# Seven-product SwiGLU pairs on one Trainium2 core: the first weight sum in two buffers of its own, and the second sum placed behind a named VectorE instruction

## The chip, the cores and the metric

The kernel runs on one core of a Trainium2 chip. The metric is device time in microseconds (us), the median of the runs shown. TensorE (PE in the profile) does the matmuls; VectorE (DVE), ScalarE (ACT) and GpSimd (POOL) each take their instructions strictly in the order in which they were queued; SP and POOL issue the transfers used here.

## The reference

A trunk of two layers over 512 tokens of width 1024, all float32. Each layer is an attention or delta-rule mixer between two half-step SwiGLU blocks, each behind an RMS norm. The part that matters here is the SwiGLU:

```python
def swiglu(h, w_gate, w_up, w_down):
    return (jax.nn.silu(h @ w_gate) * (h @ w_up)) @ w_down

for layer in range(DEPTH):          # DEPTH = 2, D_MODEL = 1024, D_FF = 2816
    x = x + 0.5 * swiglu(rms_norm(x, ffn1_norm[layer]), ffn1_w_gate[layer], ffn1_w_up[layer], ffn1_w_down[layer])
    ...                             # mixer
    x = x + 0.5 * swiglu(rms_norm(x, ffn2_norm[layer]), ffn2_w_gate[layer], ffn2_w_up[layer], ffn2_w_down[layer])
```

## The kernel before

**Blocks and pairs.** Four SwiGLU blocks run (`ffn`). Each walks the 22 column blocks of the hidden width in pairs, by groups. In the first three SwiGLU blocks the groups hold 6, 8 and 8 column blocks: the first three pairs are computed plainly (`eight`), the other eight pairs, four in each of the two later groups, by `seven`. After each group comes a down projection (`add_out`). So there are 3 x 8 = 24 pairs made by `seven`, in six groups of four. The fourth SwiGLU block doesn't use `seven`.

**The seven products.** `seven` makes a 2x2 block product with seven multiplications (a Winograd form). The halves of the depth and of the two column blocks give weight quarters; sums of quarters are formed on the way: t1 and t3 by a plain load from SP followed by an accumulating load from POOL into the same tile, t2 = t1 + b22 and t4 = t2 + b21 on VectorE (L511 and L522). Every product first splits its weights into a high and a low part (ACT cast `wh` L225, DVE subtraction `wl` L226, three buffers each) and then runs 24 matmuls of 128x256 (L498). The order of the products on TensorE is: 0 into X (b11), 1 into Y (t2), 2 into Z (t1), 3 added to Y (t3), 4 added to X (b21), 5 added to Y (t4), 6 added to Z (b22). In the profile X is an `mm` tile, Y a `pa` tile, Z a `pb` tile; `sb` is b11, `sr` holds b21 and b22.

**Reads between the products.** Y and Z are read by VectorE between products that add to them: u2 = p1 + Y after product 1 (L514), u3 = p1 + Y after product 3 (L518), c22 = Z - u3 (L504, named `gr`). Product 5 may not start on Y before u3 has read it, product 6 not on Z before c22 has. "The fourth product" below is product 3.

**Buffers.** t1, t3, t2, t4 of every pair, and the down projection's panels too, take the next of three `raw` buffers in turn, so in the kernel before t1 of the next pair can be loaded only when the buffer of the present pair's t3 is free.

**Order.** The instructions of the next pair are mixed into those of the present one by a scheduler, which sets one fixed order for each engine and each queue; `issue_after(i)` makes what stands under it come behind instruction i in that order. The norm of each SwiGLU block needs a small power on POOL (`rt`, L159) before its row scale `rb` (L299) can be made.

Of the kernel before, what the change touches and what calls it, by code (L numbers as in the profile page):

```python
# [10 lines left out]
F32 = mybir.dt.float32  # L11
F32R = mybir.dt.float32r
AF = mybir.ActivationFunctionType
ALU = mybir.AluOpType

P = 128
# [84 lines left out]
class Trunk:  # L101
# [328 lines left out]
    def quarters(self, pool):  # L430

        nc = self.nc
        tags = [(self.xp, f"xn{p}{c}") for c in range(KC) for p in "hl"]
        tags += [(pool, f"sx{i}") for i in range(12)]
        norm = []
        for kh in range(2):
            t = pool.tile([P, 4 * T], F32, tag="sr", name="xr")
            for k in range(4):  # L440
                c = kh * 4 + k
                nc.vector.scalar_tensor_tensor(t[:, k * T:(k + 1) * T], self.x[c],
                                               self.gain[:, c:c + 1], self.rb, ALU.mult, ALU.mult)
            norm.append(t.rearrange("p (k t) -> p k t", k=4))
        self.left = [[[], []] for _ in range(7)]
        v2 = lambda t: t.rearrange("p (k t) -> p k t", k=2)
        for i in range(2):
            a = [[norm[kh][:, 2 * i:2 * i + 2, t * 256:(t + 1) * 256] for kh in range(2)]
                 for t in range(2)]
            s1, s2, s3, s4 = (v2(self.small(pool, t)) for t in ("gr", "sg", "ur", "hd"))  # L450
            tt = nc.vector.tensor_tensor
            tt(s1, a[1][0], a[1][1], op=ALU.subtract)
            tt(s2, s1, a[0][0], op=ALU.subtract)
            tt(s3, a[0][0], a[1][0], op=ALU.subtract)
            tt(s4, a[0][1], s2, op=ALU.add)
            for o, src in enumerate((a[0][0], s2, s1, s3, a[0][1], a[1][1], s4)):
                h, l = (v2(pl.tile([P, T], F32R, tag=tag, name=tag, bufs=1))
                        for pl, tag in (tags.pop(0), tags.pop(0)))
                self.split_to(h, l, src)
                self.left[o][0].append(h)  # L460
                self.left[o][1].append(l)

    def seven(self, pool, wg, wu, f):

        nc = self.nc
        x8 = lambda t: t.rearrange("p (x c) -> p x c", x=8)
        def load(eng, v, kh, lo, hi, **kw):
            for q, w in enumerate((wg, wu)):  # L470
                eng.dma_start(v[:, q * 4:q * 4 + 4], w[kh * 512:(kh + 1) * 512,  # L471
                                                       f * P + lo:f * P + hi]
                              .rearrange("(k p) c -> p k c", p=P), **kw)
        raw = lambda: x8(self.wp.tile([P, 1024], F32, tag="raw", name="raw", bufs=NRAW))
        add = dict(accum_op=ALU.add)
        b11 = x8(pool.tile([P, 1024], F32, tag="sb", name="sb"))
        load(nc.sync, b11, 0, 0, P)
        b2 = x8(pool.tile([P, 2048], F32, tag="sr", name="sr"))
        load(nc.sync, b2, 1, 0, 2 * P)
        t1, t3 = raw(), raw()  # L480
        load(nc.sync, t1, 0, 0, P)
        load(nc.gpsimd, t1, 0, P, 2 * P, **add)
        load(nc.sync, t3, 0, P, 2 * P)
        load(nc.gpsimd, t3, 1, P, 2 * P, **add)
        b21, b22 = b2[:, :, :P], b2[:, :, P:]
        X, Y, Z = self.mm_ps(), self.a_ps(), self.b_ps()

        def product(ps, o, right, start=False):
            h = x8(self.wp.tile([P, 1024], F32R, tag="wh", name="wh", bufs=NSPL))
            l = x8(self.wp.tile([P, 1024], F32R, tag="wl", name="wl", bufs=NSPL))  # L490
            self.split_to(h, l, right)
            ah, al = self.left[o]
            for q in range(2):
                out = ps[:, q * 256:(q + 1) * 256]
                for k in range(4):
                    a = [t[k // 2][:, k % 2] for t in (ah, al)]
                    for i, (wt, xt) in enumerate(((h, a[0]), (h, a[1]), (l, a[0]))):
                        nc.tensor.matmul(out, lhsT=wt[:, q * 4 + k], rhs=xt,  # L498
                                         start=start and q + k + i == 0,
                                         stop=q == 1 and k == 3 and i == 2, skip_group_check=True)  # L500

        def combine(tag, a, b, op):
            t = self.small(pool, tag)
            nc.vector.tensor_tensor(t, a, b, op=op)  # L504
            return t

        product(X, 0, b11, True)
        p1 = self.np_.tile([P, T], F32, tag="acc", name="p1", bufs=1)
        nc.scalar.copy(out=p1, in_=X)
        t2 = raw()  # L510
        nc.vector.tensor_tensor(t2, t1, b22, op=ALU.add)  # L511
        product(Y, 1, t2, True)
        u2 = self.np_.tile([P, T], F32, tag="sq", name="u2")
        nc.vector.tensor_tensor(u2, p1, Y, op=ALU.add)  # L514
        product(Z, 2, t1, True)
        product(Y, 3, t3)
        u3 = self.np_.tile([P, T], F32, tag="sq", name="u3")
        nc.vector.tensor_tensor(u3, p1, Y, op=ALU.add)  # L518
        c22 = combine("gr", Z, u3, ALU.subtract)
        product(X, 4, b21)  # L520
        t4 = raw()
        nc.vector.tensor_tensor(t4, t2, b21, op=ALU.add)  # L522
        product(Y, 5, t4)
        c21 = combine("ur", p1, Y, ALU.add)
        product(Z, 6, b22)
        c12 = combine("ur", Z, u2, ALU.subtract)
        for lo, hi in ((X, c21), (c12, c22)):
            sg, hd = self.small(pool, "sg"), self.small(pool, "hd")
            for i, c in enumerate((lo, hi)):
                s = slice(i * 256, (i + 1) * 256)  # L530
                self.last_act = nc.scalar.activation(sg[:, s], c[:, :256], AF.Silu)
                nc.vector.tensor_tensor(hd[:, s], sg[:, s], c[:, 256:], op=ALU.mult)
            yield hd
# [606 lines left out]
    def gdn_base(self, pool, G, Ks):  # L1140


        nc = self.nc
        n = BASE
        iud = self.dram.tile([2 * HPITCH], F32, tag="iud", name="iud", bufs=2)
        for j, K in enumerate(Ks):
            nc.scalar.dma_start(self.rows_of(iud, j), K["iu"].rearrange("p (t s) -> p t s", s=P))
        lb = pool.tile([P, n, n], F32, tag="lb", name="lb", bufs=1)
        rr = pool.tile([P, n // 4, n], F32, tag="rr", name="rr", bufs=1)
        tmp = pool.tile([P, 9 * n], F32, tag="tmp", name="tmp", bufs=1)  # L1150
        quarters = [slice(q * 2 * NBLK, (q + 1) * 2 * NBLK) for q in range(4)]
        for s in quarters:
            nc.scalar.dma_start(lb[s], self.blocks_of(iud))
        nc.scalar.copy(out=rr, in_=G["eye"])
        for j in range(n - 1):
            m, k = n - 1 - j, j // 4 + 1
            sh = [P, k, m]
            p = tmp[:, :k * m].rearrange("p (a b) -> p a b", b=m)
            nc.gpsimd.tensor_tensor(p, rr[:, :k, j:j + 1].broadcast_to(sh),  # L1159
                                    lb[:, j, j + 1:].rearrange("p (o m) -> p o m", o=1)  # L1160
                                    .broadcast_to(sh), op=ALU.mult)
            nc.gpsimd.tensor_tensor(rr[:, :k, j + 1:], rr[:, :k, j + 1:], p, op=ALU.subtract)  # L1162
            yield
        for q, s in enumerate(quarters):
            nc.scalar.dma_start(self.blocks_of(G["rd"], q, 4), rr[s])
        for j, K in enumerate(Ks):
            K["r"] = pool.tile([P, T], F32, tag="r", name="r", bufs=3)
            nc.scalar.dma_start(K["r"].rearrange("p (t s) -> p t s", s=P), self.rows_of(G["rd"], j))
        yield
# [156 lines left out]
```

## Time and profile before

| | |
|---|---|
| median of 3 runs | 2078.2 us (2077.97 to 2080.44) |
| the profiled execution | 2081.11 us, its span 2079.3 us |
| mean granted TensorE clock | 0.980 of full speed |
| PE busy | 1992.8 us, 96% of the span |
| DVE / ACT / POOL busy | 1302.3 / 897.7 / 256.0 us |
| HBM traffic | 110 GB/s over the span |

The span runs from the first to the last instruction; the execution's own time is 1.8 us longer. Busy PE includes time in which matmuls ran at half clock.

### The profile page before, as it was taken

What the parts mean: (1) busy time and instruction counts of PE and PEld (TensorE: products, weight loads), DVE (VectorE), ACT (ScalarE), POOL (GpSimd) and SP (SyncE); (2) the same over time, 40 slices, a digit from 0 to 9 for tenths busy, and PEclk for the clock granted to TensorE, in tenths of its full rate; (3) what the DMA queues carried; (4) which work ended last, traced back from release to release, by engine and by line L of the source; (5) the groups of instructions that cost most, each with busy time, mean ns of one, the idle gap of its engine ahead of it and who ended that gap; (6) DMA issues with size and microseconds to landing.
All of it is one profiled execution on the core that took longest, in us unless ns stands there. A gap on an engine that the chain in (4) does not pass through costs nothing.

```text
span 2079.3 us, 29425 instructions
## 1 busy us (share of the span) xinstructions
PE 1992.8 (96%) x11514; PEld 1741.8 (84%) x11514; DVE 1302.3 (63%) x2058; ACT 897.7 (43%) x1577; POOL 256.0 (12%) x394
## 2 busy tenths in 40 slices
PE   8999989999889999999999998999889999999998
PEld 7889888889768899899888988977777888888887
DVE  6767466697557767476576746669667675443443
ACT  5434234455875334244333424455455553322322
POOL 0021120100000121220002112004333400000000
PEclk9999999999999999999999999999999999999999
DMA  4576463222113575563357647235323323323322
GB/s 154 159 135 173 109 134 98 89 83 70 41 62 111 150 153 153 111 133 102 99 154 137 169 108 146 92 96 139 85 64 95 79 87 103 101 91 92 101 95 78
DMA packets 291263, 230.28 MB, mean 111 GB/s; under 512 B 31618, under 2 KB 266420, under 8 KB 291124
## 3 DMA queue, kind: packets, MB, share of 16 engines
q1 hardware_dynamic: 209604, 195.21, 30.7%
q0 software_dynamic: 50688, 25.17, 9.9%
q10 hardware_dynamic: 30832, 8.02, 1.7%
q8 instruction: 90, 1.47, 0.3%
q14 instruction: 49, 0.40, 0.1%
HBM read 223.10 MB, written 5.26 MB: 110 GB/s over the span
## 4 chain that ended last, share of the span: by engine, by line
PE 53%; DMA 6%; POOL 5%; DVE 3%; issue 2%; ACT 1%; ACTq 0%; DVEq 0%; POOLq 0%; SPq 0%
PE pa L498 5%; PE pa L182 5%; PE pa L180 5%; PE pa L181 5%; PE pb L182 5%; PE pb L180 5%; PE pb L181 5%; PE mm L95 4%; DMA raw<-in_ffn_w_up_dram 4%; PE pb L498 3%; PE mm L498 3%; PE mm L181 3%; PE mm L180 3%; PE mm L182 3%; POOL tmp L1159 2%; POOL rr L1162 2%
## 5 line engine op out<-in xcount | busy, mean ns | idle before, releaser
L174 DVE TENSOR_TENSOR wl<-raw,wh 128x1024 fp32r<-128x1024 f32 (+1 forms) x252 | 295.5, 1173 | 275.2 <-ACT wh L173 274.4
L173 ACT CAST wh<-raw 128x1024 fp32r<-128x1024 f32 (+1 forms) x252 | 254.3, 1009 | 425.6 <-PE pb L181 153.5
L225 ACT CAST wh<-raw 128x1024 fp32r<-128x1024 f32 x96 | 100.8, 1050 | 186.2 <-PE pb L498 54.5
L180 PE MATMUL mm<-xnh,wh 128*128 128x512 f32 (+1 forms) x432 | 169.3, 395 | 7.7 <-DVE qT L660 5.6
L182 PE MATMUL mm<-xnh,wl 128*128 128x512 f32 (+1 forms) x432 | 169.9, 394 | 0.0
L181 PE MATMUL mm<-xnl,wh 128*128 128x512 f32 (+1 forms) x432 | 168.8, 391 | 0.0
L226 DVE TENSOR_TENSOR wl<-raw,wh 128x1024 fp32r<-128x1024 f32 x96 | 117.5, 1224 | 73.2 <-ACT wh L225 73.2
L471 POOL DMA_DIRECT2D raw<-in_ffn_w_gate_dram x48 | 67.8, 1412 | 698.0 <-DMA raw<-in_ffn_w_gate_dram 330.0
L498 PE MATMUL pa<-xnh,wh 128*128 128x256 f32 x288 | 87.0, 302 | 39.5 <-DVE u L518 38.2
L95 PE MATMUL mm<-xnh,wh 128*128 128x512 f32 x256 | 109.4, 427 | 12.5 <-DVE cx L1048 12.5
L498 PE MATMUL pa<-sx,wh 128*128 128x256 f32 x576 | 118.0, 298 | 0.0
L180 PEld LDWEIGHTS mm<-xnh,wh 128*128 128x128 f32 x432 | 83.2, 193 | 25.9 <-DVE qT L660 6.0
L181 PE MATMUL pa<-hid,wh 128*128 128x512 f32 x264 | 102.8, 389 | 0.0
L182 PE MATMUL pa<-hid,wl 128*128 128x512 f32 x264 | 102.7, 389 | 0.0
L181 PE MATMUL pb<-hid,wh 128*128 128x512 f32 x264 | 102.7, 389 | 0.0
L182 PE MATMUL pb<-hid,wl 128*128 128x512 f32 x264 | 102.7, 389 | 0.0
L180 PE MATMUL pa<-hid,wh 128*128 128x512 f32 x264 | 102.3, 389 | 0.0
L180 PE MATMUL pb<-hid,wh 128*128 128x512 f32 x264 | 102.2, 389 | 0.0
L95 PE MATMUL mm<-xnl,wh 128*128 128x512 f32 x256 | 101.8, 398 | 0.0
L95 PE MATMUL mm<-xnh,wl 128*128 128x512 f32 x256 | 101.7, 397 | 0.0
L498 PEld LDWEIGHTS pa<-sx,wh 128*128 128x128 f32 x576 | 97.5, 208 | 0.0
L182 PEld LDWEIGHTS mm<-xnh,wl 128*128 128x128 f32 x432 | 83.3, 193 | 16.3 <-issue 0.8
(391 smaller groups left out, 5543.7 us busy)
## 6 DMA issues: line engine op xcount, KB each, us to landing
raw<-in_ffn_w_down_dram SPq DMA_DIRECT2D x88, 512.0 KB, 3.7
raw<-in_ffn_w_gate_dram SPq DMA_DIRECT2D x40, 512.0 KB, 3.6
raw<-in_ffn_w_up_dram SPq DMA_DIRECT2D x40, 512.0 KB, 3.6
raw<-in_gdn_w_in_dram SPq DMA_DIRECT2D x32, 512.0 KB, 3.9
sr<-in_ffn_w_gate_dram SPq DMA_DIRECT2D x24, 512.0 KB, 3.8
sr<-in_ffn_w_up_dram SPq DMA_DIRECT2D x24, 512.0 KB, 5.0
raw<-in_ffn_w_gate_dram SPq DMA_DIRECT2D x48, 256.0 KB, 4.2
raw<-in_ffn_w_up_dram SPq DMA_DIRECT2D x48, 256.0 KB, 4.3
```

The costliest lines, as they stand in the source:

```text
L95: return self.tc.keep_in_program_order(self.engine.matmul(*args, **kw))
L173: nc.scalar.copy(out=h[:, :n], in_=raw[:, :n])
L174: nc.vector.tensor_tensor(l[:, :n], raw[:, :n], h[:, :n].bitcast(F32), op=ALU.subtract)
L180: self.te.matmul(out, lhsT=lh, rhs=rh, start=start, stop=False)
L181: self.te.matmul(out, lhsT=lh, rhs=rl, start=False, stop=False)
L182: self.te.matmul(out, lhsT=ll, rhs=rh, start=False, stop=stop)
L225: nc.scalar.copy(out=h, in_=src)
L226: nc.vector.tensor_tensor(l, src, h.bitcast(F32), op=ALU.subtract)
L471: eng.dma_start(v[:, q * 4:q * 4 + 4], w[kh * 512:(kh + 1) * 512, f * P + lo:f * P + hi] .rearrange("(k p) c -> p k c", p=P), **kw)
L498: nc.tensor.matmul(out, lhsT=wt[:, q * 4 + k], rhs=xt, start=start and q + k + i == 0, stop=q == 1 and k == 3 and i == 2, skip_group_check ...
L1159: nc.gpsimd.tensor_tensor(p, rr[:, :k, j:j + 1].broadcast_to(sh), lb[:, j, j + 1:].rearrange("p (o m) -> p o m", o=1) .broadcast_to(sh), o ...
L1162: nc.gpsimd.tensor_tensor(rr[:, :k, j + 1:], rr[:, :k, j + 1:], p, op=ALU.subtract)
```

## The change

t1 gets two buffers of its own (tag `t1`, in a pool with two buffers for each tag), and the `raw` buffers are taken in turn by t3, t2 and t4 only. The sum t2 of a pair is put behind c22 of the pair before, in VectorE's order; the first pair of a SwiGLU block has nothing to stand behind.

```diff
         self.left = [[[], []] for _ in range(7)]
+        self.met = None
...
-        t1, t3 = raw(), raw()
+        t1, t3 = x8(pool.tile([P, 1024], F32, tag="t1", name="t1")), raw()
         load(nc.sync, t1, 0, 0, P)
         load(nc.gpsimd, t1, 0, P, 2 * P, **add)
...
         t2 = raw()
-        nc.vector.tensor_tensor(t2, t1, b22, op=ALU.add)
+        with self.tc.issue_after(self.met) if self.met else nullcontext():
+            nc.vector.tensor_tensor(t2, t1, b22, op=ALU.add)
...
-        c22 = combine("gr", Z, u3, ALU.subtract)
+        c22 = self.small(pool, "gr")
+        self.met = nc.vector.tensor_tensor(c22, Z, u3, op=ALU.subtract).ins
```

VectorE, second pair of the first `seven` group going over into the third, before the change. `u2_1368`, `u3_1426` and `gr_1428` belong to the second pair, `wl_1461` is the split of its product 5 and `wl_1491` that of its product 6; `raw_1587` is t2 of the third pair, made from its t1 (`raw_1544`), and `wl_1558` is the split of the third pair's product 0.

```order
L514 TENSOR_TENSOR u2_1368<-p1_1336,pa_1306 128x512
L226 TENSOR_TENSOR wl_1431<-sr_1292,wh_1430 128x1024
L226 TENSOR_TENSOR wl_1461<-raw_1458,wh_1460 128x1024
L511 TENSOR_TENSOR raw_1587<-raw_1544,sr_1541 128x1024
L518 TENSOR_TENSOR u3_1426<-p1_1336,pa_1306 128x512
L226 TENSOR_TENSOR wl_1491<-sr_1292,wh_1490 128x1024
L504 TENSOR_TENSOR gr_1428<-pb_1307,u3_1426 128x512
L226 TENSOR_TENSOR wl_1558<-sb_1538,wh_1557 128x1024
```

The same place after the change, where `t1_1544` is the third pair's t1 and `raw_1707` its t4:

```order
L516 TENSOR_TENSOR u2_1368<-p1_1336,pa_1306 128x512
L226 TENSOR_TENSOR wl_1431<-sr_1292,wh_1430 128x1024
L226 TENSOR_TENSOR wl_1461<-raw_1458,wh_1460 128x1024
L520 TENSOR_TENSOR u3_1426<-p1_1336,pa_1306 128x512
L522 TENSOR_TENSOR gr_1428<-pb_1307,u3_1426 128x512
L513 TENSOR_TENSOR raw_1587<-t1_1544,sr_1541 128x1024
L226 TENSOR_TENSOR wl_1491<-sr_1292,wh_1490 128x1024
L525 TENSOR_TENSOR raw_1707<-raw_1587,sr_1541 128x1024
L226 TENSOR_TENSOR wl_1558<-sb_1538,wh_1557 128x1024
```

u3 and c22 have moved ahead of the next pair's t2, and t4 of the next pair has come up from further back.

SP's transfers around the second and third pair, before (`raw_1295` and `raw_1296` are t1 and t3 of the second pair, `raw_1544` and `raw_1545` those of the third; `sb_1787` and `sr_1790` belong to the fourth):

```order
L471 DMA raw_1295<-in_ffn1_w_gate_dram 128x4x128
L471 DMA raw_1295<-in_ffn1_w_up_dram 128x4x128
L471 DMA raw_1296<-in_ffn1_w_gate_dram 128x4x128
L471 DMA raw_1296<-in_ffn1_w_up_dram 128x4x128
L471 DMA sr_1541<-in_ffn1_w_gate_dram 128x4x256
L471 DMA sr_1541<-in_ffn1_w_up_dram 128x4x256
L471 DMA sb_1787<-in_ffn1_w_gate_dram 128x4x128
L471 DMA sb_1787<-in_ffn1_w_up_dram 128x4x128
L471 DMA raw_1544<-in_ffn1_w_gate_dram 128x4x128
L471 DMA raw_1544<-in_ffn1_w_up_dram 128x4x128
```

The same stretch after; `t1_1544` is the third pair's and `t1_1793` the fourth's:

```order
L472 DMA raw_1296<-in_ffn1_w_gate_dram 128x4x128
L472 DMA raw_1296<-in_ffn1_w_up_dram 128x4x128
L472 DMA t1_1544<-in_ffn1_w_gate_dram 128x4x128
L472 DMA t1_1544<-in_ffn1_w_up_dram 128x4x128
L472 DMA sr_1541<-in_ffn1_w_gate_dram 128x4x256
L472 DMA sr_1541<-in_ffn1_w_up_dram 128x4x256
L472 DMA sb_1787<-in_ffn1_w_gate_dram 128x4x128
L472 DMA sb_1787<-in_ffn1_w_up_dram 128x4x128
L472 DMA raw_1545<-in_ffn1_w_gate_dram 128x4x128
L472 DMA raw_1545<-in_ffn1_w_up_dram 128x4x128
L472 DMA t1_1793<-in_ffn1_w_gate_dram 128x4x128
L472 DMA t1_1793<-in_ffn1_w_up_dram 128x4x128
```

The load of t1 has moved ahead by one pair: beside t3 of a pair now stands t1 of the pair after it, no longer that pair's own. POOL adds in the same order.

POOL, at the start of the third SwiGLU block (`rt_9597` is its norm's power; the two tiles are t1 of its first two pairs), after the change:

```order
L472 DMA t1_10240<-in_ffn1_w_gate_dram 128x4x128
L472 DMA t1_10240<-in_ffn1_w_up_dram 128x4x128
L472 DMA t1_10489<-in_ffn1_w_gate_dram 128x4x128
L472 DMA t1_10489<-in_ffn1_w_up_dram 128x4x128
L159 TENSOR_TENSOR rt_9597<-ms_9595,halfFalse_87 128x4
```

Before, `rt_9597` stood ahead of all of this block's adds; now the adds of the first two pairs' t1 stand ahead of it, and so in each of the three SwiGLU blocks that use `seven`.

## Rows read from the trace of the kernel before

**Rows 1.** The page, busy time of each engine over the span.
```profile
PE 1992.8 (96%) x11514; PEld 1741.8 (84%) x11514; DVE 1302.3 (63%) x2058; ACT 897.7 (43%) x1577; POOL 256.0 (12%) x394
```
**Rows 2.** Groups by form: busy us, mean ns | idle us before, what ended it.
```profile
L173 ACT CAST wh<-raw 128x1024 fp32r<-128x1024 f32 x228 | 239.5, 1051 | 397.7 <-PE pb L181 153.5 <-PE mm L181 65.5 <-PE pb L182 63.2
...
L498 PE MATMUL pa<-xnh,wh 128*128 128x256 f32 x288 | 87.0, 302 | 39.5 <-DVE u L518 38.2 <-ACT sg L531 1.3
...
L511 DVE TENSOR_TENSOR raw<-raw,sr 128x1024 f32<-128x1024 f32 x24 | 29.4, 1225 | 85.6 <-DMA raw<-in_ffn_w_up_dram 70.5 <-issue 15.0
```
**Rows 3.** Waits: total us, times, longest us.
```profile
PE pa L498 <- DVE u L518: 38.2, 17, 3.8
```
**Rows 4.** Timeline of DVE around the second wait of a group: start, us.
```profile
765.62 1.22 DVE L226 TENSOR_TENSOR wl<-raw,wh 128x1024 fp32r<-128x1024 f32 x1 [1.66 <-ACT wh L225]
770.80 1.23 DVE L511 TENSOR_TENSOR raw<-raw,sr 128x1024 f32<-128x1024 f32 x1 [3.96 <-DMA raw<-in_ffn_w_up_dram]
771.95 0.68 DVE L518 TENSOR_TENSOR u<-p,pa 128x512 f32<-128x512 f32 x1
772.54 1.22 DVE L226 TENSOR_TENSOR wl<-sr,wh 128x1024 fp32r<-128x1024 f32 x1
773.68 0.68 DVE L504 TENSOR_TENSOR gr<-pb,u 128x512 f32<-128x512 f32 x1
```
**Rows 5.** Timelines of SP, POOL and ACT: one t1, then one t3.
```profile
760.35 0.37 SPq L471 DMA_DIRECT2D raw<-in_ffn_w_gate_dram  x1
...
764.73 1.84 POOL L471 DMA_DIRECT2D raw<-in_ffn_w_up_dram  x1
...
761.45 0.37 SPq L471 DMA_DIRECT2D raw<-in_ffn_w_gate_dram  x1
...
758.78 1.05 ACT L225 CAST wh<-raw 128x1024 fp32r<-128x1024 f32 x1 [0.99 <-ACT sg L531]
```
**Rows 6.** The chain that ended last, pieces in order of time: start, us, what.
```profile
749.95 3.11 PE pa L498 x24
...
755.94 2.88 PE mm L498 x24
...
772.77 4.61 PE pa L498 x24
...
807.16 2.88 PE pa L498 x24
...
1164.06 5.46 PE pa L498 x24
```
**Rows 7.** Windows, the six groups of four pairs: length, busy by engine, clock, DMA.
```profile
115.50:204.07 88.57, 82.65 (x673) 82.12 (x672) 63.13 (x76) 39.32 (x53) 15.64 (x12) 0.98 0.70 160
...
sum 545.57, PE 506.08 PEld 502.92 DVE 378.89 ACT 238.51 POOL 93.86; mean PE 84.35 PEld 83.82 DVE 63.15 ACT 39.75 POOL 15.64
```
**Rows 8.** Windows between the ends of successive waits, same columns.
```profile
749.95:772.77 22.82, 20.38 (x168) 20.21 (x169) 16.29 (x21) 10.61 (x16) 5.21 (x4) 1.00 0.82 168
772.77:796.80 24.03, 21.87 (x168) 21.70 (x169) 16.39 (x21) 10.19 (x14) 5.20 (x4) 0.93 0.72 151
```
**Rows 9.** DMA issues: KB each, median us from issue to landing.
```profile
raw<-in_ffn_w_up_dram SPq DMA_DIRECT2D x48, 256.0 KB, 4.3
...
raw<-in_ffn_w_up_dram POOLq DMA_DIRECT2D x48, 256.0 KB, 6.3
```
**Rows 10.** Timelines of SP, POOL and DVE at SwiGLU block starts.
```profile
18.39 0.37 SPq L471 DMA_DIRECT2D sb<-in_ffn_w_gate_dram  x1
...
33.27 1.95 POOL L159 TENSOR_TENSOR rt<-ms,halfFalse 128x4 f32<-128x4 f32 x1 [31.96 <-DVE ms L277]
...
40.69 0.69 DVE L299 COPY rb<-pa 128x512 f32<-128x512 f32 x1 [3.86 <-PE pa L296]
...
1002.03 0.37 SPq L471 DMA_DIRECT2D sb<-in_ffn_w_gate_dram  x1
...
1019.45 1.88 POOL L159 TENSOR_TENSOR rt<-ms,halfFalse 128x4 f32<-128x4 f32 x1 [92.33 <-DVE ms L277]
```

## The prediction

> **What bounds the kernel now.** First the page: PE is busy 96% of the span [rows 1], so only two things can save time here, PE's idle time and the stretches in which its clock is low. Then the groups by form, sorted for idle time in front of PE: one group of seven-product matmuls, those that write `pa`, has 39.5 us of idle ahead of it, nearly all ended by VectorE's `u` at L518, which is u3 [rows 2]. The list of waits gives 17 such waits, the longest 3.8 us [rows 3]; with the one that the groups put down to ACT (1.3 us) that makes 18. Eighteen is also what the code gives: six groups of four pairs, and in each group three pairs that have a next pair mixed into them.
>
> Then VectorE's timeline at one of the 18. After the split of product 5 (765.62) VectorE stands 3.96 us, until POOL's add into t1 of the next pair has landed; then it makes t2 (770.80), then u3 (771.95), and at 772.77 product 5 starts [rows 4, 6]. u3 itself needed nothing but product 3. That had ended near 767.45: PE's wait here is 22.82 - 20.38 = 2.44 us [rows 8], product 4 before it takes 2.88, and 772.77 - 2.44 - 2.88 = 767.45. u3 was held for 4.5 us only because it was queued behind t2. So the wait on the path is a transfer's: t1 was loaded from 760.35 on, POOL's second add went out at 764.73, and t2 began at 770.80, 10.45 us after the first load [rows 4, 5]. It was loaded that late because its buffer is that of the present pair's t3.
>
> Last, the chain that ended last shows what a wait costs beyond its idle time. A product of 24 matmuls takes 2.88 us, on `mm` and on `pa` alike; the product 5 behind a wait takes 3.11, 4.61 or, at worst, 5.46 us [rows 6]. The clock column says why: the pair behind the shorter wait has a granted clock of 1.00, the pair behind the next, 2.44 us long, 0.93 [rows 8]: the clock fell to its lower level, 1.2 GHz, for a few us and came back.
>
> **The change part by part.** *What the 18 waits cost now.* The six groups last 545.57 us, in which PE is busy 506.08 [rows 7]. A pair without any wait would take 7 products of 2.88 us = 20.16 us, four of them 80.64, six groups 483.84. The excess is 545.57 - 483.84 = 61.7 us. Of it 545.57 - 506.08 = 39.5 us is idle (the same 39.5 as in rows 2), and 506.08 - 483.84 = 22.2 us is busy time too long: 18 x 0.23 = 4.1 us for filling the pipeline anew (3.11 - 2.88), and 18.1 us of lower clock.
>
> *u3 and c22 ahead of t2.* In the new order u3 follows the split of product 5 directly, and that split was done at 766.8, before the stall began. I walk one pair from the end of product 3 (0 us), with PE running through: product 4 is over at 2.88, 5 at 5.76, 6 at 8.64. VectorE needs 0.6 us for each 512-wide piece and 1.14 for each 1024-wide one when they follow each other (771.95, 772.54, 773.68 in rows 4). u3 starts a few tenths after 0 and is done at 1.0; product 5 wants it at 2.88. c22 is done at 1.6, t2 of the next pair at 2.8, the split of product 6 at 3.9; product 6 wants it at 5.76. Both have 1.9 us to spare. VectorE's whole work for a pair is 16.3 us [rows 8] against 20.16, so it doesn't become the bound; ACT's is 10.2 to 10.6.
>
> *What is queued behind t2 now.* Everything of VectorE from the split of product 6 on, and through it PE. So t2's operands decide: if they land more than 1.9 us after t2's turn, product 6 stalls in place of product 5. Their new dates: t3 of a pair is loaded about when it is now (761.45, the split that frees its buffer doesn't move), the t1 of the pair after behind it, 0.9 us later. On POOL t3's two adds go first, some 3 us. With today's 10.45 us that t1 lands 14.4 us after t3's load was issued, and that load goes out 6.0 us ahead of a product 3's end (761.45 against 767.45): t1 lands at 8.4 us. The t2 that needs it stands behind the c22 of the following pair, at 20.16 + 1.6 = 21.8. That is 13 us of lead where there were -4. `sr`, the other operand, is loaded in the same place as before, and its wait isn't among those of L511. t3 lands at -6.0 + 10.45 = 4.4 us, and its cast is wanted one period after the one at 758.78, at -8.7 + 20.16 = 11.5: 7 us of lead [rows 5]. So this part costs nothing as long as the leads hold, and the 61.7 us go.
>
> t4, which comes forward to a place behind the split of product 6, costs nothing either: VectorE has 3.9 us free in a period (20.16 - 16.3), and the next split behind it, that of the coming product 0, is still done at 3.9 + 2 x 1.14 = 6.2, wanted at 8.64. On PE the first two matmuls of the coming product 0 now stand inside product 6; they want only its cast, which can start when product 4 gives its buffer back (2.88) and takes some 1.05 us [rows 2], so it is there before 5.76.
>
> *Block starts.* Three times t1 of the first two pairs is now loaded at the very start, 1 MB more, and its four adds stand on POOL ahead of the norm's `rt`. In the third block the `sb` loads start at 1002.03; eight loads of about 0.5 us each are out by 1006, and at 4.3 us for landing, twice that when they crowd, POOL has issued the last add by about 1018; `rt` is at 1019.45 [rows 9, 10]. At the first block the last load is out near 25 (18.39 and the panels between), and POOL is free near 34 to 35 where `rt` began at 33.27; but the row scale waits 3.86 us for PE's slot there [rows 10], so 1 to 2 us are covered. If that cover is gone each us costs a us. The panels that follow the extra loads come later by what 1 MB takes, 6 us at the 168 GB/s of rows 8; their casts wait for PE, not for DMA, in every large releaser of their row [rows 2]. I take 1.5 us in all for the three starts, from 0 to 6.
>
> *Sum.* -61.7 + 1.5 = -60.2 us. The profiled execution took 2081.1 us, so 2020.9; it lay 2.9 us over the median, so against the median of 2078.2 us the forecast is 2018 us.
>
> **The rivals.** *The clock doesn't come back.* Eighteen holes are gone, but the clock could still dip. For it: how long it stays low differs from wait to wait (4.61 and 5.46 us for the product behind [rows 6]), so more than one thing may set it. Against it: the pairs behind the shorter waits run at 1.00 throughout [rows 8]. Then only 39.5 + 4.1 go: 2078.2 - 43.6 + 1.5 = 2036 us. The Trainium skill speaks for this rival (TensorE: Matmul & The Clock Gate, "A second HAM failure mode: psum-queue depth-cycling"): short idle stretches between groups of matmuls can keep the clock moving between its two levels. By that rule the time is this rival's; rows 8 agree only where the wait was the longer one.
>
> *The stall moves to t2 or t3.* The same bytes of a pair (168 GB/s x 22.82 us = 3.8 MB) now have to pass in 20.16 us. The DMA engines are busy 0.82 of 22.82 us now, 18.7 us [rows 8], so 0.93 of a period. If crowding doubles the 10.45 us of a chain, t3 comes 3 to 4 us late (its lead is 7) and t2 still in time. Say half of the 61.7 us then stay as a new wait: 2078.2 - 30.9 = 2047 us. Against it: a fourth pair of each group loads little, so the queue can run empty. The Trainium skill bears on this (DMA: Bandwidth & Descriptors, "Queues, rings and completion order"): each DMA engine takes its queues in turn, packet by packet, so POOL's adds and SP's loads slow each other. No row here shows it apart; the longer landing of POOL's adds, 6.3 us against 4.3 [rows 9], doesn't contradict it.
>
> *Slower than before.* One mechanism can do it: t2 stands in front of the splits of products 6, 0 and 1, so a late t1 now blocks more than u3. The price per pair is the lateness beyond 1.9 us, with the same clock loss behind it. It is worse than today from 3.4 us of stall (61.7 / 18) on, so when t1 lands over 1.6 + 1.9 + 3.4 = 6.9 us after product 3, some 19 us later than worked out (20.16 + 6.9 against 8.4). That happens if SP or POOL hold t1 back by nearly a pair, behind a transfer that waits for a buffer. At 5 us of stall in all 18: 2078.2 + 18 x 1.6 = 2107 us.
>
> *Nothing happens*, because product 5 waited for something other than u3, for instance the cast of its weights: 2078 us. The timeline speaks against it: product 5 began 0.14 us after u3 ended.
>
> **How the numbers follow.** Full relief 0.76 (2014 to 2025), clock stays 0.07, half relief 0.11, nothing 0.03, slower 0.03. 0.2% of this kernel is about 4 us, and a measurement can hardly tell less. Faster 0.94, same 0.03, slower 0.03. The range runs from 2013 (the whole 61.7 gone, and 3 us for the spread of the runs) to 2036, which takes in the clock rival and leaves the half relief out.
>
> **What the profile of the changed kernel would show.** Right: idle ahead of product 5 near zero; u3 directly behind the split of product 5, and t2 starting with no wait for a DMA; every product 5 in 2.88 us, a clock of 1.00 in the six groups, each near 80.6 us long; a busy DMA share near 0.9. Wrong: idle in VectorE's t2, ended by a DMA, with PE waiting for the split of product 6 (the late operand); a cast of t3's weights that waits for a DMA, ahead of product 3; a clock below 1 with no hole (the first rival); PE idle at the block starts behind `rb`.

## The result, and the profile after

| | before | after |
|---|---|---|
| median | 2079.1 us (4 runs, 2078.0 to 2080.4) | 2019.1 us (4 runs, 2018.6 to 2019.7) |
| span of the profiled execution | 2079.3 us | 2016.9 us |
| mean granted TensorE clock | 0.980 | 0.992 |

The ratio is 0.971 (95% interval 0.969 to 0.973): 60 us faster, where 2018 us was forecast. On the page, PE's busy time fell by 25 us although it runs the same 11514 matmuls, and the span by 62 [rows 1]:

```profile
PE 1967.6 (98%) x11514; PEld 1720.1 (85%) x11514; DVE 1304.0 (65%) x2058; ACT 897.3 (44%) x1577; POOL 254.6 (13%) x394
```

The groups by form (busy us, mean ns | idle us before, what ended it) that answer to [rows 2]: product 5's first matmuls and t2, now at L513.

```profile
L499 PE MATMUL pa<-xnh,wh 128*128 128x256 f32 x288 | 81.5, 283 | 0.0
...
L513 DVE TENSOR_TENSOR raw<-t,sr 128x1024 f32<-128x1024 f32 x24 | 29.2, 1216 | 0.1
```

The 39.5 us of idle time are gone, the mean of one matmul fell from 302 to 283 ns, and t2, which had 85.6 us of idle time ahead of it, has 0.1. VectorE's timeline at the second transition of the third group, the place of [rows 4]:

```profile
741.32 1.23 DVE L226 TENSOR_TENSOR wl<-raw,wh 128x1024 fp32r<-128x1024 f32 x1 [1.66 <-ACT wh L225]
743.19 0.69 DVE L520 TENSOR_TENSOR u<-p,pa 128x512 f32<-128x512 f32 x1 [0.64 <-PE pa L499]
743.91 0.69 DVE L522 TENSOR_TENSOR gr<-pb,u 128x512 f32<-128x512 f32 x1
744.52 1.21 DVE L513 TENSOR_TENSOR raw<-t,sr 128x1024 f32<-128x1024 f32 x1
745.65 1.22 DVE L226 TENSOR_TENSOR wl<-sr,wh 128x1024 fp32r<-128x1024 f32 x1
746.79 1.22 DVE L525 TENSOR_TENSOR raw<-raw,sr 128x1024 f32<-128x1024 f32 x1
```

u3 now waits for nothing but product 3 (PE `pa`); t2 and the two pieces behind it follow with no gap. The chain that ended last, products 4 and 5 of this pair, and windows of the six groups (the first and the sum) and of one pair, as in [rows 6 to 8] (length, busy by engine, clock, DMA share, GB/s):

```profile
743.15 2.88 PE mm L499 x24
746.03 2.88 PE pa L499 x24
```

```profile
114.95:195.47 80.52, 80.52 (x673) 80.52 (x672) 62.33 (x75) 39.27 (x53) 18.23 (x14) 1.00 0.84 183
...
sum 483.12, PE 483.12 PEld 483.10 DVE 373.63 ACT 238.10 POOL 93.61; mean PE 80.52 PEld 80.52 DVE 62.27 ACT 39.68 POOL 15.60
```

```profile
725.87:746.03 20.16, 20.16 (x171) 20.16 (x170) 16.47 (x21) 10.19 (x15) 5.21 (x4) 1.00 0.89 184
```

PE is busy from the first to the last us of every group, at the upper clock. The groups became 545.57 - 483.12 = 62.45 us shorter, the span 2079.3 - 2016.9 = 62.4. Nothing was gained or lost elsewhere.

### The profile page after: what moved, and what is told of

Its sections match the earlier page's. It is cut to its first block, busy times and chain, and to the rows that moved or that the text cites. A ratio compares the mean times of both kernels' runs of the same rounds, so it can differ in the third digit from the quotient of the medians.

```text
span 2016.9 us, 29447 instructions
## 1 busy us (share of the span) xinstructions
PE 1967.6 (98%) x11514; PEld 1720.1 (85%) x11514; DVE 1304.0 (65%) x2058; ACT 897.3 (44%) x1577; POOL 254.6 (13%) x394
## 4 chain that ended last, share of the span: by engine, by line
PE 60%; POOL 5%; DMA 2%; DVE 2%; issue 1%; ACT 1%; ACTq 0%; POOLq 0%; DVEq 0%
PE pa L499 7%; PE pa L182 5%; PE pa L180 5%; PE pa L181 5%; PE pb L182 5%; PE pb L180 5%; PE pb L181 5%; PE mm L95 5%; PE pb L499 5%; PE mm L499 5%; PE mm L181 3%; PE mm L182 3%; PE mm L180 3%; POOL tmp L1162 2%; POOL rr L1165 2%
## 5 line engine op out<-in xcount | busy, mean ns | idle before, releaser
L226 DVE TENSOR_TENSOR wl<-raw,wh 128x1024 fp32r<-128x1024 f32 x72 | 88.0, 1223 | 79.0 <-ACT wh L225 79.0
L225 ACT CAST wh<-raw 128x1024 fp32r<-128x1024 f32 x72 | 75.5, 1049 | 113.6 <-PE pb L499 43.9
L499 PE MATMUL pa<-sx,wh 128*128 128x256 f32 x576 | 109.9, 283 | 0.0
L472 POOL DMA_DIRECT2D raw<-in_ffn_w_gate_dram x24 | 30.9, 1289 | 561.0 <-DMA raw<-in_ffn_w_gate_dram 306.8
L181 PEld LDWEIGHTS mm<-xnl,wh 128*128 128x128 f32 x432 | 82.8, 192 | 15.6 <-issue 0.2
L225 ACT CAST hid<-hd 128x512 fp32r<-128x512 f32 x88 | 54.5, 619 | 81.3 <-DVE hd L427 72.9
```

Of the source, the lines that this page charges most:

```text
L181: self.te.matmul(out, lhsT=lh, rhs=rl, start=False, stop=False)
L225: nc.scalar.copy(out=h, in_=src)
L226: nc.vector.tensor_tensor(l, src, h.bitcast(F32), op=ALU.subtract)
L499: nc.tensor.matmul(out, lhsT=wt[:, q * 4 + k], rhs=xt, start=start and q + k + i == 0, stop=q == 1 and k == 3 and i == 2, skip_group_check ...
```

## The experiments

Two questions were open. The change has two halves, the place of t2 and the buffers of t1: which of them does it? And is a hole ahead of product 5 enough to lower the clock, or does that take the late transfer? Eight kernels ran in two sets of four, each with the kernel before beside it, whose median was 2081.3 us (9 runs, 2075.3 to 2086.8) for the first set and 2084.9 (9 runs, 2074.9 to 2086.3) for the second. Edits are against the changed kernel.

**Order alone.**

```diff
-        t1, t3 = x8(pool.tile([P, 1024], F32, tag="t1", name="t1")), raw()
+        t1, t3 = raw(), raw()
```

> Half of the change: t2 of the next pair stands behind c22 as in the change, but t1 stays in the three raw buffers and is loaded as late as before. My theory (u3 was the victim of its place behind a late t1; what is late now stands in front of product 6, which has 1.9 us to spare): before, t1 landed some 3.4 us after product 3's end, and t2's turn is at 1.6 us, so VectorE waits 1.8 to 2.8 us in t2 and product 6 is late by 0 to 0.9 us. 0 to 18 times 1.1 us (0.9 idle and 0.23 refill) = 0 to 20 us over the changed kernel: 2019 to 2039 us, likeliest 2028, with DVE idle ahead of t2 still 30 to 50 us in 18 pairs. Rival A (the lateness is only handed on, product 6 waits as long as product 5 did): about 2060 to 2080 us, with 35 to 40 us idle ahead of the pb products. Rival B (the order alone does it all, buffers don't matter): 2019 us and no wait for a DMA in t2.

Measured: 2022.9 us, ratio 0.972 (0.970 to 0.9735). Groups by form, product 6's matmuls (those with the low part of the weights wait first) and t2:

```profile
L499 PE MATMUL pb<-xnh,wl 128*128 128x256 f32 x192 | 55.1, 287 | 3.3 <-DVE wl L226 3.3
...
L513 DVE TENSOR_TENSOR raw<-raw,sr 128x1024 f32<-128x1024 f32 x24 | 29.4, 1226 | 50.8 <-DMA raw<-in_ffn_w_up_dram 36.6 <-issue 14.3
```

One t2, and the matmul of product 6 that it holds up:

```profile
769.96 1.23 DVE L513 TENSOR_TENSOR raw<-raw,sr 128x1024 f32<-128x1024 f32 x1 [2.83 <-DMA raw<-in_ffn_w_up_dram]
...
772.37 0.39 PE L499 MATMUL pb<-xnh,wl 128*128 128x256 f32 x1 [0.70 <-DVE wl L226]
```

t2 still stands 36.6 us waiting for its transfers, in 21 waits of up to 2.8 us, but only 3.3 us of it reach PE. The kernel is some 3 us slower than the one with the buffers alone (below), not 20 or 60. So a late transfer was not what cost the 62 us: it cost them because u3 stood behind it. Rival A falls by the time. Rival B falls by the waits, though its time was nearly right.

**Buffers alone.**

```diff
-        with self.tc.issue_after(self.met) if self.met else nullcontext():
-            nc.vector.tensor_tensor(t2, t1, b22, op=ALU.add)
+        nc.vector.tensor_tensor(t2, t1, b22, op=ALU.add)
```

> The other half: t1 has its two buffers of its own, t2 is not tied to c22. In the order that follows, t2 stands ahead of u2, and t4 of the next pair stands directly ahead of u3, where t2 stood before. My theory (the wait was the transfer's, the place ahead of u3 costs little when the operand is there): t2 finds its t1 landed, t4 takes 1.14 us in time in which VectorE has nothing else, u3 is late by at most 1.1 us of its 1.9: 2018 to 2021 us, no idle ahead of product 5. Rival (the place ahead of u3 is what costs, any 1024-wide piece there delays product 5): 0.5 to 1.1 us with 0.23 of refill in 18 pairs, 2032 to 2043 us, and DVE u as the releaser of pa products.

Measured: 2020.0 us, ratio 0.9706 (0.969 to 0.972), the same as the change. VectorE's timeline at the same place:

```profile
740.52 1.23 DVE L226 TENSOR_TENSOR wl<-raw,wh 128x1024 fp32r<-128x1024 f32 x1 [1.07 <-ACT wh L225]
741.78 1.22 DVE L524 TENSOR_TENSOR raw<-raw,sr 128x1024 f32<-128x1024 f32 x1
742.93 0.68 DVE L519 TENSOR_TENSOR u<-p,pa 128x512 f32<-128x512 f32 x1
```

Here a sum as wide as t2 (it is t4) stands directly ahead of u3, as t2 did before. It has its operands, so it runs in time in which VectorE would have waited for product 3, and u3 starts in time; PE has no idle time ahead of any seven-product matmul. The rival falls. Either half is enough: they are two cures of one wait, and their gains don't add.

**One buffer for t1.**

```diff
-        t1, t3 = x8(pool.tile([P, 1024], F32, tag="t1", name="t1")), raw()
+        t1, t3 = x8(pool.tile([P, 1024], F32, tag="t1", name="t1", bufs=1)), raw()
```

> The change with one buffer for t1 in place of two: t1 of the next pair is loaded when product 2 of the present pair has split its weights, a whole pair later than in the change. From the trace of the changed kernel: the load goes out 8.8 us ahead of product 3's end, POOL's second add 4.0 us ahead, and an add lands some 6 us after its issue, so t1 lands about 2 us after product 3's end, t2's turn is at 1.6. My theory (only lateness beyond 1.9 us costs): VectorE waits 0 to 1.5 us in t2, product 6 not at all: 2017 to 2022 us, the same as the change; the second buffer is worth nothing in time. Rival (the lead of nearly a pair is needed, because landings scatter): a third or more of the 18 pairs stall by 1 us or more, over 2028 us.

Measured: 2036.0 us, ratio 0.978 (0.976 to 0.980). My theory's number was wrong here. POOL's add into t1, VectorE's timeline at the second transition of the first group, and the PE row of that moment:

```profile
145.08 2.73 POOL L472 DMA_DIRECT2D t<-in_ffn_w_up_dram  x1
...
147.03 0.69 DVE L520 TENSOR_TENSOR u<-p,pa 128x512 f32<-128x512 f32 x1 [0.64 <-PE pa L499]
147.75 0.69 DVE L522 TENSOR_TENSOR gr<-pb,u 128x512 f32<-128x512 f32 x1
152.48 1.23 DVE L513 TENSOR_TENSOR raw<-t,sr 128x1024 f32<-128x1024 f32 x1 [4.04 <-DMA t<-in_ffn_w_up_dram]
153.62 1.22 DVE L226 TENSOR_TENSOR wl<-sr,wh 128x1024 fp32r<-128x1024 f32 x1
...
154.90 0.39 PE L499 MATMUL pb<-xnh,wl 128*128 128x256 f32 x1 [1.67 <-DVE wl L226]
```

t2 waits 4.04 us, 18 times 2.7 us on the mean (1.0 to 4.1); I had 0 to 1.5. At this transition POOL issued t1's second add at 145.08 and t2 could start at 152.48, so the add took 7.4 us where I took 6. It also went out some 2 us later than I took: 1.95 us ahead of u3 (147.03), not 4.0 us ahead of product 3's end. The rival's time came, over 2028 us, and its stalls in part: twelve of the 18 pairs stalled, five of them by 1 us or more. The mechanism holds: in these twelve pairs PE waited 2.37 us less than t2 did (4.04 and 1.67 here, 3.65 and 1.28, 2.46 and 0.09), and none where t2 waited under 2.4 us. With the order alone the same difference is 2.13 us (2.83 and 0.70, 2.52 and 0.39). That is the margin which the prediction worked out as 1.9 us, measured twice. So with the order in place a second buffer is worth some 16 us, and one buffer of its own is worse than none (2036.0 us for 2022.9). In the shared ring t1's load and adds go ahead of t3's; here they stand behind them, on SP and on POOL. That this is the cause was not tried apart.

**A hole that no transfer causes, short.**

```diff
-        nc.vector.tensor_tensor(u3, p1, Y, op=ALU.add)
+        for _ in range(3):
+            nc.vector.tensor_tensor(u3, p1, Y, op=ALU.add)
```

> The changed kernel with u3 computed three times in place of once in all 24 pairs (the same sum into the same tile; work added, none left out): a delay of product 5 that no transfer causes. Two of the three stand behind the split of product 5, then the split of product 6, then the third: 0.2 + 2 x 0.6 + 1.14 + 0.6 + 0.1 = 3.25 us after product 3's end, where product 5 wants it at 2.88. My theory: 24 holes of about 0.4 to 0.5 us, each with 0.23 us of refill, no lower clock behind so short a hole: 2019 + 24 x 0.65 = 2034 us (2030 to 2040), clock as in the change (0.99). Rival (any hole ahead of product 5 lowers the clock): 1.0 us more for each, 2058 us, and a mean clock of 0.98 or less. Rival 2 (the margin is larger than worked out): 2019 us.

Measured: 2039.6 us, ratio 0.980 (0.978 to 0.9815), clock 0.991.

```profile
L499 PE MATMUL pa<-xnh,wh 128*128 128x256 f32 x288 | 83.1, 289 | 15.1 <-DVE u L521 15.1
```

24 holes of 0.63 us, longer than the 0.4 to 0.5 that I had, and with them a span of 2037.8 - 2016.9 = 20.9 us more: 15.1 idle and 5.8, or 0.24 us each, for the restart. The 0.23 of the prediction is confirmed, and there is no room for a clock loss of 1 us. Both rivals fall.

**The same in steps.** The coming product 0 is held behind c22, and u3 is computed four, five, six and eight times:

```diff
-        product(X, 0, b11, True)
+        with self.tc.issue_after(self.met) if self.met else nullcontext():
+            product(X, 0, b11, True)
...
-        nc.vector.tensor_tensor(u3, p1, Y, op=ALU.add)
+        for _ in range(4):      # 5, 6, 8
+            nc.vector.tensor_tensor(u3, p1, Y, op=ALU.add)
```

> The changed kernel with u3 computed four times in place of once in all 24 pairs (the same sum into the same tile; work added), and the coming product 0 held behind c22: a hole ahead of product 5 that no transfer causes, one step of 0.6 us longer than with three times. Hole by the last run (0.69 us): 1.3 us. My theory (the time behind a hole is lost to the clock only where the hole is near 2 us or longer, as behind the 18 waits of before, where holes up to 1.8 us cost nothing behind them): 24 x (1.3 + 0.2) = 36 us over 2020: 2056 us, mean clock 0.99. Rival (the clock loss of before came from something else than the hole's length, and any hole of a microsecond has it too): 24 x 1.2 more, 2085 us.

> The same with u3 computed five times. A piece of the activation now stands between and waits for ScalarE until about 4.3 us after product 3's end, so the hole is about 2.4 us, the mean length of the waits of before. My theory: behind most of these holes the clock falls as it did before (1.2 us lost on the mean), 24 x (2.4 + 0.2 + 1.2) = 91 us: 2111 us (2095 to 2120), mean clock 0.98. Rival (a hole alone doesn't lower the clock, it was the late transfers or VectorE's stop with it): 24 x 2.6 = 62 us: 2082 us, clock 0.99.

> The same with u3 computed six times: hole about 3.0 us. My theory: behind the longest waits of before (3.1 and 3.8 us) 2.4 to 2.6 us were lost, so 24 x (3.0 + 0.2 + 2.0) = 125 us: 2145 us (2120 to 2160), mean clock 0.97. Rival (no clock loss without a late transfer): 24 x 3.2 = 77 us: 2097 us, clock 0.99.

> The same with u3 computed eight times: hole about 4.2 us. My theory, with the loss behind a hole no longer growing in proportion: 24 x (4.2 + 0.2 + 2.6) = 168 us: 2188 us (2170 to 2210), mean clock 0.96. Rival (no clock loss without a late transfer): 24 x 4.4 = 106 us: 2126 us, clock 0.99.

| u3 computed | median, us | ratio (95% interval) | span over after, us | idle ahead of these products, us | clock |
|---|---|---|---|---|---|
| 4 times | 2052.5 | 0.985 (0.983 to 0.988) | 32.8 | 24.4 | 0.992 |
| 5 times | 2094.8 | 1.006 (1.004 to 1.0075) | 75.6 | 39.4 | 0.978 |
| 6 times | 2102.9 | 1.010 (1.007 to 1.012) | 85.9 | 52.4 | 0.980 |
| 8 times | 2154.0 | 1.034 (1.032 to 1.037) | 137.9 | 78.4 | 0.963 |

The holes are not shaped as I meant. In 18 of the 24 pairs two matmuls of the coming product 0 stand ahead of product 5 on PE and wait 1.02 us for their cast, and u3's wait follows them. PE rows of one pair with u3 computed five times, and the window from there to the next such place:

```profile
774.54 0.38 PE L499 MATMUL mm<-xnh,wh 128*128 128x256 f32 x1 [1.02 <-ACT wh L225]
...
775.87 0.39 PE L499 MATMUL pa<-xnh,wh 128*128 128x256 f32 x1 [0.83 <-DVE u L522]
```

```profile
775.87:799.89 24.02, 22.16 (x168) 21.75 (x169) 19.12 (x25) 10.20 (x14) 5.24 (x4) 0.93 0.72 150
```

The groups by form of that kernel. The last row counts too: in the fourth pair of a group no next pair is mixed in, and the down projection's first matmuls stand there.

```profile
L499 PE MATMUL pa<-xnh,wh 128*128 128x256 f32 x288 | 88.9, 309 | 15.0 <-DVE u L522 15.0
L499 PE MATMUL mm<-xnh,wh 128*128 128x256 f32 x288 | 83.3, 289 | 18.3 <-ACT wh L225 18.3
...
L180 PE MATMUL pa<-hid,wh 128*128 128x512 f32 x264 | 103.0, 392 | 6.1 <-ACT wh L173 6.1
...
L514 DVE TENSOR_TENSOR raw<-t,sr 128x1024 f32<-128x1024 f32 x24 | 29.3, 1219 | 0.1
```

This kernel has the idle time of the kernel before without its late transfer, though in other holes: 39.4 us idle where before had 39.5, t2 with no wait (0.1), and a lower clock all the same. Of the 36.2 us that are not idle some 10 are restarts (42 at about 0.25), the rest is clock, as the window's 0.93 says, the same 0.93 as behind a wait of before [rows 8]. So a hole is enough, and the rival without a late transfer falls (2082 against 2094.8). With four computations, one hole of 1.02 us in a pair, no loss to the clock shows (0.35 us for each of 24 holes beside the idle time, clock 0.992 as in the changed kernel); with eight, a window shows 0.88:

```profile
803.48:830.77 27.29, 23.28 (x168) 22.87 (x168) 21.36 (x28) 10.20 (x14) 5.21 (x4) 0.88 0.64 135
```

The forecasts of my theory for five and eight computations were too high, 2111 and 2188 us, and mostly because less idle time came than I took: 39.4 and 78.4 us for 58 and 101. The kernel with six computations decides against the rest of my theory: 2103 us, far under its 2120 to 2160. Of the 42 us to its likeliest 2145, 20 are idle time that didn't come (52.4 us for 72); the rest is clock. What stands behind a hole can be summed from PE's timeline, as the time by which the starts of matmuls lie further apart than 0.12 us until the next hole. With five computations (1.02 and 0.84 us idle) 15 of 18 pairs lose 1.3 to 1.6 us; with six (1.02 and 1.55) only 11 lose, 1.3 to 2.8, and seven lose under 0.3; with eight (1.02 and 3.0) all 18 lose 2.1 to 2.8. The loss doesn't simply grow with the hole. What else sets it stays open.

## Why the prediction was right

**The excess of 61.7 us.** 62.45 went, in its parts 39.5 idle and 506.08 - 483.12 = 22.96 busy. The prediction's 22.2 is 0.7 lower because it took 80.64 us for a group, and the windows show 80.52. All of the 22.96 went with the holes; the experiment with short holes confirms its restart term (0.24 against 0.23), the one with five computations that the clock term belongs to holes. Summed from PE's timeline as above, the eleven pairs of before that lost time to the clock lost some 18 us, the prediction's 18.1.

**Why t1 was loaded late.** Here the text ahead and the prediction are wrong: t1 did not wait for the buffer of the present pair's t3. SP's waits and VectorE's timeline of before, at the place of [rows 5]:

```profile
SPq L471 <- DVE raw L522: 153.0, 18, 11.2
```

```profile
759.07 1.22 DVE L522 TENSOR_TENSOR raw<-raw,sr 128x1024 f32<-128x1024 f32 x1
760.20 1.22 DVE L226 TENSOR_TENSOR wl<-raw,wh 128x1024 fp32r<-128x1024 f32 x1
```

The load of t1 at 760.35 went out when the sum t4 (L522), the last reader of the present pair's t2, had ended at 760.29. The split of t3 ended only at 761.42, and the load of the next t3, at 761.45, followed that. So t1 took the buffer of t2, and the late place of t4 held it back. The change cures this too, since t1 leaves the ring. Whether an earlier t4 alone would have been a third cure was not tried.

**u3 and c22 ahead of t2.** This came as the prediction walked it. u3 ends 743.88 and product 5 starts 746.03: a margin of 2.15 us for the 1.9 worked out. The split of product 6 ends at 746.87, and the runs with a late t2 give 2.1 to 2.4 us for its margin.

**What is queued behind t2.** t2's operand is there: idle 0.1 us. The leads are larger than worked out. Timelines of VectorE, SP, POOL and ACT, for one t3 and one t1:

```profile
730.16 1.22 DVE L226 TENSOR_TENSOR wl<-raw,wh 128x1024 fp32r<-128x1024 f32 x1
...
731.40 0.37 SPq L472 DMA_DIRECT2D raw<-in_ffn_w_gate_dram  x1
...
734.16 0.37 SPq L472 DMA_DIRECT2D t<-in_ffn_w_gate_dram  x1
...
736.96 1.75 POOL L472 DMA_DIRECT2D raw<-in_ffn_w_up_dram  x1
...
738.58 2.75 POOL L472 DMA_DIRECT2D t<-in_ffn_w_up_dram  x1
...
754.63 1.05 ACT L225 CAST wh<-raw 128x1024 fp32r<-128x1024 f32 x1 [0.75 <-ACT sg L534]
```

t3's load goes out 11.75 us ahead of product 3's end (743.15), not 6.0: the step "the split that frees its buffer doesn't move" was wrong: without t1 in the ring it is t3 that takes the buffer of t2, and its load follows the split of product 1 (730.16 to 731.38), not that of product 3. By the median landings of POOL's adds (5.9 and 6.6 us) t3 lands near 742.9 and t1 near 745.2; t3's cast runs at 754.63, t2 one period after 744.52 at 764.68. That is an estimate of 12 us of lead for t3 and 19 for t1, where 7 and 13 were forecast. The error was on the safe side.

**Block starts.** 1.5 us were taken, from 0 to 6; it was nothing. Outside the six groups before took 2079.3 - 545.57 = 1533.7 us and after 2016.9 - 483.12 = 1533.8. POOL and VectorE at the first block:

```profile
32.13 1.69 POOL L472 DMA_DIRECT2D t<-in_ffn_w_up_dram  x1
32.90 1.99 POOL L159 TENSOR_TENSOR rt<-ms,halfFalse 128x4 f32<-128x4 f32 x1
...
40.10 0.69 DVE L299 COPY rb<-pa 128x512 f32<-128x512 f32 x1 [3.61 <-PE pa L296]
```

The four adds were out just in time: `rt` stands directly behind the last, at 32.90 where it began at 33.27 before, and the row scale still waits for PE's slot, 3.61 us for 3.86 [rows 10]. The estimate had POOL free at 34 to 35. It also counted 1 MB more for each start; with the four adds, 256 KB each like the loads [rows 9], it is 2 MB, and even that cost nothing that shows.

**The sum.** In spans 62.4 us went, where 60.2 were forecast. The medians fell by 60.0 only, because the profiled execution of before lay 2.0 us over its median and that of after 0.5 us under. And 0.9 of the 1.1 us between 2018 and the measured 2019.1 is the starting point, a median of 2078.2 over three runs that is 2079.1 over the four. So that the number came this near is in part luck: the sum was 2.2 us too small, and the place of the two profiled executions hides it.

**The rivals.** The clock didn't stay low: 1.00 in all six groups. The Trainium skill's rule (TensorE: Matmul & The Clock Gate, "A second HAM failure mode: psum-queue depth-cycling") is about gaps, so it doesn't speak for a clock that stays low without them, as the prediction had it. With the gaps gone no trace here shows its effect; where gaps were put back, five computations and up, it shows (mean clock 0.963 to 0.980). The stall didn't move to t2 or t3: the DMA share of the pair shown is 0.89, near the 0.93 worked out, and nothing waits for it. What the prediction didn't see is that either half of the change would have done; it priced them as one.

## What to carry to other kernels

A wait that the list puts down to an engine's result may be a transfer's, one instruction further up in that engine's queue: look at what stands ahead of the late instruction and what that waited for. There are then two cures, to bring the transfer forward or to put the urgent instruction ahead of the waiting one; price each alone, since here both at once gave no more than one, and the waiting instruction may wait as long as the work behind it has margin. The idle time that a list shows is not all that a hole costs; here the restart and the lower clock behind it came to more than half as much again.

## What the runs showed of the hardware that was not expected

**Equal holes don't cost the same.** In the trace of before, five holes of 0.8 to 1.8 us ahead of product 5 lost nothing behind them; of eleven between 1.85 and 2.6 us nine lost 1.3 to 1.6 us and two nothing (2.33 and 2.59 us); the two over 3 us lost 2.4 and 2.6. PE's rows of two of them, and their windows:

```profile
1140.53 0.36 PE L498 MATMUL pa<-xnh,wh 128*128 128x256 f32 x1 [2.59 <-DVE u L518]
...
1274.93 0.36 PE L498 MATMUL pa<-xnh,wh 128*128 128x256 f32 x1 [2.41 <-DVE u L518]
```

```profile
1140.53:1164.06 23.53, 20.39 (x169) 20.22 (x169) 16.29 (x21) 10.20 (x14) 5.24 (x4) 0.97 0.74 157
1274.93:1299.17 24.24, 21.87 (x168) 21.69 (x169) 16.38 (x21) 10.20 (x14) 5.22 (x4) 0.93 0.65 131
```

Behind the longer hole PE is busy 20.39 us with the same seven products, behind the shorter one 21.87. (The 0.97 of the first window comes from its end, ahead of the next product: up to 1162.50 the clock is 1.00.) What makes the difference stays open.

**Two short holes lowered the clock where one did not.** One hole of 1.02 us in a pair lost nothing to the clock (0.992); 1.02 and 0.84 us with two matmuls between them lowered the clock in 15 of 18 pairs.
